# A hybrid decoder layer on one core: attention without the shifted copy of V, its remainders turned in 64x64 products

## The chip, the core and the metric

The kernel runs on one core of one Trainium2 chip, in one launch. The metric is the device time of a run in microseconds. A core has a matrix engine (TensorE, PE in the profile, with its weight loads as PEld), a vector engine (VectorE, DVE), an engine for activation functions (ScalarE, ACT), a general engine (GpSimd, POOL), an engine that issues transfers (SyncE, SP), and 16 DMA engines that serve the queues of SP, ACT and POOL. PE reads operands from SBUF and writes PSUM, 128 partitions in eight banks.

## The reference, cut to what matters

The layer projects x (2048 x 1024), runs an attention of 16 heads and a state-space mixer on the projections, gates and normalises both, and projects the result back. The change is in the attention, which is done for the dilations 1, 4 and 16 and then mixed by their log sums:

```python
def dilated_window_attention(q, k, v, slopes, dilation):
    # query t attends to t - j*dilation, j = 0..128; positions are split into
    # `dilation` residue sequences, each in blocks of 128; own and previous block
    scores = einsum('bnqrhe,bnkrhe->bnrhqk', qb, kk)
    valid = (jk >= 0) & (steps >= 0) & (steps <= ATT_STEPS)
    scores = where(valid, scores - slopes * steps * dilation, -inf)
    lse = logsumexp(scores, axis=-1)
    o = einsum('bnrhqk,bnkrhe->bnqrhe', exp(scores - lse), vv)
    return o, lse
...
    wts = softmax(stack([l1, l2, l3]), axis=0)
    y_att = wts[0] * o1 + wts[1] * o2 + wts[2] * o3
    y_att = rms_norm(y_att * silu(z_att), att_norm_g)
...
    out = einsum('bse,ed->bsd', concatenate([y_att, y_ssm], axis=-1), w_out)
    x = layer_norm(alpha * x + out, ln_g, ln_b)
```

All arithmetic is float32. A query in a block of 128 sees its own block up to itself and the previous block from the same place on.

## The kernel before, in words

Up to about 1148 us the kernel does the input projection and the mixer. It leaves q, k, v, the gate and the mixer's results in DRAM, and the output weights split in two parts (`d_wo`). The change leaves that alone.

**Pairs, dilations, units.** The attention then goes over eight pairs of heads (`pr`). A pair has three passes `d`: 0 for dilation 16, 1 for dilation 4, 2 for dilation 1. A pass has 16 blocks of 128 queries, in four groups `qd` of four; a *unit* (`pr, d, qd, half`) takes two of the four (`2 * i + half`, i = 0, 1), for both heads. There are 8 x 3 x 4 x 2 = 192 units. `first` (L902) says that a block has no previous block: all of dilation 16, the group `qd` = 0 of dilation 4, and block 0 of dilation 1.

**The window.** A block is worked in two halves `a` of 64 queries. With a previous block each half sees 192 keys: the first half those from two half blocks back, the second half those from one half block back. Of these, 128 are turned and multiplied as a whole, and 64 are left: the *remainder*. In the kernel before, both halves take the 192 keys in order of position (`keys`, L925), and the product of the first 128 with V needs 128 rows of V that start in the middle of a block for one of the halves. For that a second, shifted copy of V (`vs`, loaded at L880) stands beside V: row p of its block m is row p + 64 of V.

**The five steps of a unit.** `scores` (L935) multiplies q and k in 64x64 tiles (64 features of one head, 64 queries of one half), 192 or 128 columns each; head h writes its own PSUM bank. DVE adds the table of biases and takes the row minimum (L953). `exponentials` (L957) runs on ACT. `transposes` (L972) turns the probabilities on PE: four 128x128 transposes for the whole parts (L976), and, where a block has a remainder, two 128x128 transposes for the remainders (L984), which lie side by side in columns 128 to 256 because `cols` (L920) puts the second block's columns at the end of the tile. DVE copies both results to SBUF (PT L978, PC L987). `values` (L990) multiplies with V: products of 128 keys by 64 features (PT), then products of 64 keys (PC), which are added to the first. It accumulates into two PSUM tiles N0 and N1, one for each block index `i`; after two units ACT (or DVE) copies them out to `num` (L1022 to L1034).

**The order of the work** is written out by hand (L1254 to L1342): iteration i issues the scores of unit i, the transposes of unit i - 2 and the values of unit i - 3, in this order on PE. Between them, at fixed places `at` of the unit i - 3, stand the steps of the pair before: statistics to DRAM, `weights`, `broadcast` (L1083, on Sync's queue), `combine` (L1099, on POOL, for the last pair on DVE), and `keep_u` (L1095), which stores a pair's gated result in DRAM from a tile of the ring `wb` of three. A memset on DVE (L1087) opens each later use of this ring. V is loaded a pass at a time from POOL's or Sync's queue (L1302 to L1304, and the table STEPS at L1245).

**The output stage** (from L1343) computes the 16 row blocks of the result in two branches of eight 128x512 weights each, the mixer's (`br` = 1, weights 8 to 15) first. `load_w` (L1137) loads weights from POOL's queue into tiles that the attention has freed; LOADS (L1248) says where in the last pair each is loaded, `None` for a whole tile of 1 MB and 0 for the first half of it. The second halves of 12 to 15 are loaded behind the last unit (L1296). The last pair's broadcast and combination lie in this stage too, and the splits of the mixer's rows (L1159) stand behind them on DVE. PE's products of this stage are L1201 to L1203.

## Time and profile before

| what | value |
|---|---|
| median of three runs | 2009.96 us (2007.39 to 2012.77) |
| the profiled execution | 2003.82 us |
| its span, first to last instruction | 2002.0 us |
| mean granted PE clock | 0.991 |
| busy share of the span: PE, DVE, ACT, POOL | 97%, 64%, 56%, 50% |
| moved by DMA | 447.67 MB, 224 GB/s |

The profile is of one execution. Its times are microseconds from the span's start unless marked ns; L947 is line 947 of the kernel. A row of the timeline has the start, the length, the engine, the line, the operation, what it writes and reads, the shape, and how many instructions are merged in it; in brackets the engine's idle time before it and what ended that. A row of groups has the count, then busy time and mean ns of one, then the idle time before. PE's products are pipelined and their ends are modelled, so that PE can be busy without being at its peak; the distance from start to start says what a product occupies.

### The profile page before, as it was taken

How to read it: one execution, taken by the hardware profiler on the slowest of the kernel's cores; microseconds unless marked ns; L12 is line 12 of the kernel's file. 1: busy time of each engine (PE TensorE's matmuls, PEld its weight loads, DVE VectorE, ACT ScalarE, POOL GpSimd, SP SyncE). 2: the span in 40 equal slices, each digit the busy share in tenths (PEclk: the TensorE clock that was granted, in tenths of full speed). 3: DMA queues.
4: the chain of work that ended last, by engine and by line, in shares of the span. 5: the costliest groups of instructions: out<-in, count | busy, mean ns of one | idle time of the engine just before them, and what ended most of it. 6: DMA issues, size and time to landing. Idle time of an engine off the chain costs nothing.

```text
span 2002.0 us, 42714 instructions
## 1 busy us (share of the span) xinstructions
PE 1945.7 (97%) x16008; PEld 1588.2 (79%) x16008; DVE 1275.8 (64%) x3204; ACT 1120.0 (56%) x3036; POOL 998.3 (50%) x877
## 2 busy tenths in 40 slices
PE   8999999999999999999999999999999888999998
PEld 7888899888888888988888877777777666888886
DVE  7655376887766655644454388888887736655553
ACT  5454343566556774456566488988888732322220
POOL 0366514666556667155565343676776622432221
PEclk9999999999999999999999999999999998999999
DMA  6788676566787876888888766888888988332210
GB/s 270 236 284 293 213 280 227 159 195 190 237 306 266 279 245 239 312 269 256 272 277 259 256 228 165 229 244 235 252 238 254 265 242 260 134 102 92 92 61 32
DMA packets 260656, 447.67 MB, mean 224 GB/s; under 512 B 44785, under 2 KB 146673, under 8 KB 249057
## 3 DMA queue, kind: packets, MB, share of 16 engines
q1 hardware_dynamic: 170912, 205.39, 32.2%
q0 software_dynamic: 39088, 142.54, 21.6%
q10 hardware_dynamic: 50448, 97.01, 15.7%
q8 instruction: 126, 2.06, 0.4%
q14 instruction: 82, 0.66, 0.1%
HBM read 301.85 MB, written 151.39 MB: 226 GB/s over the span
## 4 chain that ended last, share of the span: by engine, by line
PE 85%; DVE 5%; DMA 4%; ACT 3%; issue 2%; POOL 1%; SPq 0%; ACTq 0%; DVEq 0%; POOLq 0%
PE pp L260 13%; PE pp L264 13%; PE pp L262 13%; PE N L1002 7%; PE S L947 6%; PE T L976 5%; PE pp L309 4%; PE S L1201 4%; PE S L1203 4%; PE S L1202 3%; PE ss L309 2%; PE T L1201 2%; PE T L1203 2%; PE T L1202 2%; PE ss L627 2%
## 5 line engine op out<-in xcount | busy, mean ns | idle before, releaser
L217 POOL TENSOR_TENSOR w<-wr,w 128x512 fp32r<-128x512 f32 x217 | 285.6, 1327 | 268.2 <-ACT w L216 184.0
L962 ACT ACTIVATE P<-P,st 128x192 f32<-128x192 f32 (+1 forms) x768 | 323.4, 423 | 59.9 <-DVE st L953 55.4
L252 ACT COPY ev<-pp 128x512 f32<-128x512 f32 x200 | 117.1, 587 | 315.3 <-PE pp L264 281.5
L953 DVE CUSTOM_DVE_ANT_0 P<-S,tb 128x192 f32<-128x192 f32 (+1 forms) x768 | 205.8, 324 | 53.6 <-PE S L947 44.1
L272 DVE TENSOR_TENSOR ev<-pp,ev 128x512 f32<-128x512 f32 x152 | 101.2, 686 | 140.6 <-PE pp L264 95.9
L216 ACT CAST w<-wr 128x512 fp32r<-128x512 f32 x224 | 134.1, 620 | 23.5 <-DVE wr L211 11.9
L962 ACT ACTIVATION_READ_ACCUMULATOR P<-P,st 128x1 f32 x768 | 145.0, 189 | 0.0
L1111 POOL TENSOR_TENSOR wb<-num,wb 128x2048 f32<-128x2048 f32 x21 | 95.7, 4558 | 93.7 <-DMA wb<-d_wd 90.2
L978 DVE COPY PT<-T 128x512 f32<-128x512 f32 x192 | 131.7, 686 | 3.8 <-PE T L976 3.8
L976 PE MATMUL T<-ident,P 128*128 128x128 f32 x768 | 127.3, 288 | 6.7 <-DVE PT L978 4.5
L1002 PE MATMUL N<-PT,v 128*64 128x64 f32 (+1 forms) x1536 | 124.5, 259 | 4.2 <-DVE PT L978 3.5
L976 PEld LDWEIGHTS T<-ident,P 128*128 128x128 f32 x768 | 81.3, 141 | 52.9 <-ACT P L962 16.8
L211 DVE TENSOR_TENSOR wr<-wr 128x512 f32<-128x512 f32 x128 | 112.2, 877 | 9.3 <-DMA wr<-w 5.9
L947 PE MATMUL S<-k,ex 64*64 64x192 f32 (+1 forms) x2048 | 108.8, 322 | 3.2 <-issue 3.2
L1002 PEld LDWEIGHTS N<-PT,v 128*64 128x64 f32 x1536 | 79.4, 138 | 38.3 <-issue 22.7
L459 DVE SCALAR_TENSOR_TENSOR ss<-U,cw,ss 128x512 f32<-128x512 f32 x144 | 106.0, 752 | 2.9 <-ACT ss L455 0.6
L1177 DVE TENSOR_REDUCE tb<-P 128x128 f32<-128x1024 f32 x30 | 60.2, 2006 | 45.1 <-ACT P L1174 21.1
L1239 POOL TENSOR_TENSOR k<-k,wb 128x1024 f32<-128x1024 f32 x8 | 25.8, 3225 | 122.0 <-DVE k L1238 122.0
L587 ACT ACTIVATE mt<-csb,wdr 128x128 f32<-128x128 f32 x256 | 78.9, 395 | 0.9 <-PE ss L627 0.8
L947 PEld LDWEIGHTS S<-k,ex 64*64 64x64 f32 x2048 | 66.4, 134 | 15.4 <-issue 8.9
L596 DVE TENSOR_TENSOR mt<-mt,ss 128x1024 f32<-128x1024 f32 x32 | 39.0, 1220 | 54.1 <-ACT mt L592 53.7
L260 PE MATMUL pp<-TT4h,w 128*128 128x512 f32 x176 | 69.6, 395 | 0.0
(493 smaller groups left out, 5991.1 us busy)
## 6 DMA issues: line engine op xcount, KB each, us to landing
wr<-w ACTq DMA_DIRECT2D x164, 256.0 KB
d_wc<-w SPq DMA_DIRECT2D x48, 512.0 KB
w<-d_wc POOLq DMA_DIRECT2D x48, 512.0 KB, 6.4
wb<-d_wd SPq DMA_DIRECT2D x48, 512.0 KB
d_wo<-wot POOLq DMA_DIRECT2D x32, 512.0 KB, 4.3
csb<-d_cs ACTq DMA_DIRECT2D x32, 512.0 KB
d_wv<-w SPq DMA_DIRECT2D x14, 1024.0 KB
w<-d_wv POOLq DMA_DIRECT2D x14, 1024.0 KB, 8.7
```

The costliest lines, as they stand in the source:

```text
L216: nc.scalar.copy(h, r)
L217: low.tensor_tensor(l, r, h.bitcast(F32), op=OP.subtract)
L260: nc.tensor.matmul(ps, w[:, 0, k], th[:, k], start=start and k == 0, stop=False, skip_group_check=not start)
L262: nc.tensor.matmul(ps, w[:, 0, k], tl[:, k], start=False, stop=False, skip_group_check=not start)
L264: nc.tensor.matmul(ps, w[:, 1, k], th[:, k], start=False, stop=(k == 3), skip_group_check=not start)
L309: nc.tensor.matmul(o, (th, tl)[j == 1][:, k, t], w[:, int(j == 2), k], start=start and r % 2 == k == j == 0, stop=(k == 3 and j == 2), ski ...
L947: nc.tensor.matmul(o, A["q"][d][64 * h:64 * h + 64, blk, 64 * a:64 * a + 64], kv, start=True, stop=True)
L953: nc.vector.tensor_tensor_reduce(P[:, h, cs], sp[h][:, cs], t, -0.125, 3.0e38, OP.add, OP.min, accum_out=stat(A, 0, d, h, blk))
L962: nc.scalar.activation(p, p, AF.Exp, bias=stat(A, 0, d, h, blk), scale=-1.0, accum_out=stat(A, 1, d, h, blk))
L976: nc.tensor.transpose(tp[:, h, i], P[:, h, 256 * i:256 * i + 128], ident)
L978: nc.vector.tensor_copy(pt, tp)
L1002: nc.tensor.matmul(o, l, r, start=start, stop=True, skip_group_check=True)
```

## The change

Six edits belong together:

- `keys` returns parts. Where a block has a previous one, the first half takes its 192 keys in order as before; the second half takes its own block (128 keys) first and the 64 keys of the previous block as a part of its own, written behind them. So both halves' first 128 columns belong to keys that start at a block of V. `scores` issues the first parts of both heads and halves, then the second parts. `cols` puts the second block's columns at 192, and the table of biases follows the new order.
- `transposes` turns the remainders in 64x64 products with a 64x64 piece of the identity, one for each head, block and half, with the result of half `a` in rows 64a to 64a + 63. They are plain products, not transposes.
- `values` keeps one accumulator for each half `a` in place of one for each block. First blocks of dilations 4 and 1 are done in two halves as well. The copies to `num` follow the new places.
- The shifted V and its loads go.
- `keep_u` is issued at (0, 0, 1) and not at (1, 0, 0).
- The three tiles of the shifted V take the weights 8, 9 and 10, in pairs 5 and 6; 11, 12 and 13 are loaded whole in the last pair, from its second pass on; 14 and 15 follow with their first halves, and the first half of weight 2 of the other branch. Behind the last unit only the second halves of 14 and 15 are left.

```diff
         def cols(d, qd, half, i):
-            w = 128 if first(d, qd, 2 * i + half) else 192
-            return slice(384 - w, 384) if i else slice(0, w)
+            return slice(192 * i, 192 * i + (128 if first(d, qd, 2 * i + half) else 192))
 
         def keys(A, d, qd, bq, h, a):
...
-            lo, hi = (j, j + 2 * w) if f else (j + w * (a - 2), j + w * (a + 1))
-            k = k[:, 4 * bq:4 * bq + 4, lo:hi] if d == 1 else k[:, :, lo:hi]
-            return k.rearrange("p r (c j) -> p c r j", j=4)
+            parts = [(0, j, j + 2 * w)] if f else [(0, j, j + 2 * w), (128, j - w, j)] if a else [(0, j - 2 * w, j + w)]
+            at = lambda lo, hi: k[:, 4 * bq:4 * bq + 4, lo:hi] if d == 1 else k[:, :, lo:hi]
+            return [(c, c + 64 * (hi - lo) // w, at(lo, hi).rearrange("p r (c j) -> p c r j", j=4)) for c, lo, hi in parts]
...
         def scores(A, d, qd, half):
...
-                for h in range(2):
-                    for a in range(2):
-                        o, kv = sp[h][64 * a:64 * a + 64, cs], keys(A, d, qd, 2 * i + half, h, a)
...
+                for n in range(2):
+                    for h in range(2):
+                        for a in range(2):
+                            for c0, c1, kv in keys(A, d, qd, 2 * i + half, h, a)[n:n + 1]:
+                                o = sp[h][64 * a:64 * a + 64, 192 * i + c0:192 * i + c1]
...
         def transposes(d, qd, half, P):
...
-            tc_ = psT.tile([128, 2, 2, 128], F32, name="T")
+            tc_ = psT.tile([128, 2, 2, 64], F32, name="T")
             for h in range(2):
-                nc.tensor.transpose(tc_[:, 0, h], P[:, h, 128:256], ident)
-            pc = io.tile([128, 2, 128], F32, name="PC", bufs=2)
-            rows = slice(64 * new[0], 128)
-            nc.vector.tensor_copy(pc[rows], tc_[rows, 0])
+                for i in range(new.start, new.stop):
+                    for a in range(2):
+                        r = slice(64 * a, 64 * a + 64)
+                        nc.tensor.matmul(tc_[r, h, i], P[r, h, 192 * i + 128:192 * i + 192], ident[r, r],
+                                         start=True, stop=True)
+            pc = io.tile([128, 2, 2, 64], F32, name="PC", bufs=2)
+            nc.vector.tensor_copy(pc[:, :, new], tc_[:, :, new])
...
         def values(A, d, qd, half, pts):
...
+                f = first(d, qd, 2 * i + half)
+                for a in range(2):
+                    for h in range(2):
+                        mm(out(i, h, a), v[:, m if f else m - 1 + a, 64 * h:64 * h + 64],
+                           pt[:, h, i, 64 * a:64 * a + 64], half == i == 0)
...
                 for a in range(2):
                     for h in range(2):
-                        w = (v, vs)[a != i][:, m - (a == i == 0 or a != i), 64 * h:64 * h + 64]
-                        mm(out(i, h, 64 * a, 64 * a + 64), w, pt[:, h, i, 64 * a:64 * a + 64], half == 0 and a == 0)
...
+                        r = slice(64 * a, 64 * a + 64)
+                        mm(out(i, h, a), v[r, at(2 * i + half) - a, 64 * h:64 * h + 64], pc[r, h, i], False)
...
-        LOADS = {(1, 0, 0): ((8, None, "k_0"),), (1, 1, 0): ((9, None, "q_0"),), (1, 2, 0): ((11, None, "vs"),),
-                 (1, 3, 0): ((12, 0, "q_1"), (13, 0, "v")), (2, 1, 0): ((10, None, "ex"),),
-                 (2, 2, 0): ((14, 0, "v"), (15, 0, "vs"))}
+        LOADS = {(5, 2, 1, 0): ((8, None, "vs"),), (6, 0, 1, 0): ((9, None, "vs"),), (6, 2, 1, 0): ((10, None, "vs"),),
+                 (7, 1, 0, 0): ((11, None, "k_0"),), (7, 1, 1, 0): ((12, None, "q_0"),), (7, 1, 3, 0): ((13, None, "q_1"),),
+                 (7, 2, 0, 0): ((14, 0, "v"),), (7, 2, 1, 0): ((15, 0, "v"),), (7, 2, 2, 0): ((2, 0, "ex"),)}
...
                         if pr == 7:
-                            for e in range(12, 16):
+                            for e in (14, 15):
                                 load_w(e, 1)
...
-                        load_v(pairs[pr], "v", 2, nc.sync)
-                        load_v(pairs[pr], "vs", 2, nc.sync)
+                        load_v(pairs[pr], 2, nc.sync)
...
-                    if pr > 1 and at == (1, 0, 0):
+                    if pr > 1 and at == (0, 0, 1):
                         keep_u(pairs[pr - 2], nc.sync)
...
-                    for e, name in enumerate(("num", "vs", "v", "wb", "num", "wb", "num")):
-                        load_w(1 + e, 0, name)
+                    for e, name in enumerate(("num", None, "v", "wb", "num", "wb", "num")):
+                        if name:
+                            load_w(1 + e, 0, name)
...
-        k = 64 * (p[:, None] // 64 + c[None, :] // 64 - 2) + kw[c % 64][None, :]
+        k = 64 * (p[:, None] // 64 + (c[None, :] // 64 + p[:, None] // 64) % 3 - 2) + kw[c % 64][None, :]
```

More of the change, by code (lines that the diff above doesn't have):

```diff
@@ L975, in transposes @@
                 for i in range(2):
-                    nc.tensor.transpose(tp[:, h, i], P[:, h, 256 * i:256 * i + 128], ident)
+                    nc.tensor.transpose(tp[:, h, i], P[:, h, 192 * i:192 * i + 128], ident)
             pt = io.tile([128, 2, 2, 128], F32, name="PT", bufs=4)
             nc.vector.tensor_copy(pt, tp)
-            new = [i for i in range(2) if not first(d, qd, 2 * i + half)]
-            if not new:
+            new = slice(int(first(d, qd, half)), 2 - int(first(d, qd, 2 + half)))
+            if new.start >= new.stop:
                 return pt, None
-            tc_ = psT.tile([128, 2, 2, 128], F32, name="T")
+            tc_ = psT.tile([128, 2, 2, 64], F32, name="T")
             for h in range(2):
-                nc.tensor.transpose(tc_[:, 0, h], P[:, h, 128:256], ident)
-            pc = io.tile([128, 2, 128], F32, name="PC", bufs=2)
-            rows = slice(64 * new[0], 128)
-            nc.vector.tensor_copy(pc[rows], tc_[rows, 0])
+                for i in range(new.start, new.stop):
+                    for a in range(2):
+                        r = slice(64 * a, 64 * a + 64)
+                        nc.tensor.matmul(tc_[r, h, i], P[r, h, 192 * i + 128:192 * i + 192], ident[r, r],
+                                         start=True, stop=True)
+            pc = io.tile([128, 2, 2, 64], F32, name="PC", bufs=2)
+            nc.vector.tensor_copy(pc[:, :, new], tc_[:, :, new])
             return pt, pc
@@ L996, in values, with out @@
                 A["N"] = [psN.tile([128, 512], F32, name=f"N{i}") for i in range(2)]
-            num, v, vs = A["num"][d], A["v"][d], A["vs"].get(d)
+            num, v = A["num"][d], A["v"][d]
             at = lambda bq: 4 * bq + qd if d == 1 else 4 * qd + bq
-            out = lambda i, h, lo, hi: A["N"][i][64 * h:64 * h + 64, 128 * half + lo:128 * half + hi]
+            def out(i, h, a=None):
+                if d == 0:
+                    return A["N"][i][64 * h:64 * h + 64, 128 * half:128 * half + 128]
+                c = 64 * (2 * i + half)
+                return A["N"][a][64 * h:64 * h + 64, c:c + 64]
             def mm(o, l, r, start):
@@ L1004, in values @@
                 m = at(2 * i + half)
+                if d == 0:
+                    for h in range(2):
+                        mm(out(i, h), v[:, m, 64 * h:64 * h + 64], pt[:, h, i], half == 0)
+                    continue
+                f = first(d, qd, 2 * i + half)
+                for a in range(2):
+                    for h in range(2):
+                        mm(out(i, h, a), v[:, m if f else m - 1 + a, 64 * h:64 * h + 64],
+                           pt[:, h, i, 64 * a:64 * a + 64], half == i == 0)
+            for i in range(2):
                 if first(d, qd, 2 * i + half):
-                    for h in range(2):
-                        mm(out(i, h, 0, 128), v[:, m, 64 * h:64 * h + 64], pt[:, h, i], half == 0)
                     continue
@@ L1010, in values @@
                     for h in range(2):
-                        w = (v, vs)[a != i][:, m - (a == i == 0 or a != i), 64 * h:64 * h + 64]
-                        mm(out(i, h, 64 * a, 64 * a + 64), w, pt[:, h, i, 64 * a:64 * a + 64], half == 0 and a == 0)
-            for a in range(2):
-                for i in range(2):
-                    m, rows = at(2 * i + half), slice(64 * i, 64 * i + 64)
-                    if first(d, qd, 2 * i + half):
-                        continue
-                    for h in range(2):
-                        w = v[rows, m - i] if a == i else vs[rows, m - 2 * i]
-                        mm(out(i, h, 64 * a, 64 * a + 64), w[:, 64 * h:64 * h + 64],
-                           pc[rows, h, 64 * a:64 * a + 64], False)
+                        r = slice(64 * a, 64 * a + 64)
+                        mm(out(i, h, a), v[r, at(2 * i + half) - a, 64 * h:64 * h + 64], pc[r, h, i], False)
             if half == 1:
@@ L1326, in hybrid_layer @@
                             if dd:
-                                load_v(pairs[pr + nx], x, dd[0])
+                                load_v(pairs[pr + nx], dd[0])
                             else:
@@ L1331, in hybrid_layer @@
                         permute(pairs[pr + 1], 1)
+                    if not half:
+                        for e, hf, name in LOADS.get((pr, d, qd, 0), ()):
+                            load_w(e, hf, name)
                     if pr < 7:
                         continue
-                    for e, hf, name in LOADS.get(at, ()):
-                        load_w(e, hf, name)
                     if at == (2, 0, 0):
```

39 lines of the change are left out of this document (17 added, 22 removed).

## The prediction

> **What bounds the kernel now.** I read the page first, then the stretches of the attention stage and of the output stage, then the timeline of one unit, and last the waits. The page gives the span and the chain that ended last:
>
> ```profile
> span 2002.0 us, 42714 instructions
> ...
> PE 85%; DVE 5%; DMA 4%; ACT 3%; issue 2%; POOL 1%; SPq 0%; ACTq 0%; DVEq 0%; POOLq 0%
> ```
>
> TensorE (PE) carries 85% of that chain. But the change touches only the attention (192 units from about 1148 to 1613 us) and the first 60 us of the output stage, so those two are read by themselves. The columns of the stretches are busy us and count of PE, PEld, DVE, ACT, POOL, then the granted clock, DMA share and GB/s:
>
> ```profile
> 1160.00:1613.00 453.00, 432.01 (x8135) 323.00 (x8135) 376.53 (x1877) 382.27 (x1697) 289.00 (x229) 0.98 0.80 232
> ...
> 1630.00:1640.00 10.00, 10.00 (x46) 8.12 (x45) 1.82 (x4) 4.54 (x6) 0.00 (x0) 1.00 1.09 325
> 1640.00:1650.00 10.00, 7.51 (x33) 5.80 (x31) 2.29 (x1) 0.00 (x0) 0.00 (x0) 1.00 1.02 237
> 1650.00:1660.00 10.00, 0.45 (x1) 0.45 (x2) 5.72 (x3) 0.47 (x1) 4.68 (x7) 0.60 1.19 255
> ```
>
> In the attention PE is idle for 21 us of 453, DVE for 76 and ACT for 71. A busy PE is not PE at its peak, so one steady unit of a second half (dilation 1, two blocks that each have a remainder) has to be read in order of time:
>
> ```profile
> 1420.73 0.83 PE L947 MATMUL S<-k,ex 64*64 64x192 f32 x16
> ...
> 1420.96 0.41 DVE L987 COPY PC<-T 128x256 f32<-128x256 f32 x1
> ...
> 1421.49 0.42 PEld L976 LDWEIGHTS T<-ident,P 128*128 128x128 f32 x4 [0.28 <-DVE PC L987]
> 1421.50 0.66 PE L976 MATMUL T<-ident,P 128*128 128x128 f32 x4
> ...
> 1421.99 0.38 PE L984 MATMUL T<-ident,P 128*128 128x128 f32 x2
> ...
> 1422.31 0.34 PE L1002 MATMUL N<-PT,v 128*64 128x64 f32 x4
> ...
> 1422.92 0.27 PE L1002 MATMUL N<-PC,v 64*64 64x64 f32 x2
> ...
> 1423.20 0.83 PE L947 MATMUL S<-k,ex 64*64 64x192 f32 x16
> ```
>
> The unit lasts 1423.20 - 1420.73 = 2.47 us and PE's four blocks fill it: scores 0.77 us, turning (L976 with L984) 0.81, values 0.61, remainders 0.28. The gap of 0.28 us in front of L976 is put down to DVE's copy of PC, but that copy ended at 1421.37, before L976 began: what shows is a pause that comes each time the tile size of the products changes (64x64, 128x128, 128x64, 64x64). So PE paces these units, and what is added to PE's work there is added to the time.
>
> **The change part by part.** *The remainders' turning.* Before, a unit turns its remainders in two 128x128 transposes (L984); after, in eight products of 64x64 with the identity. How many records such a product makes is seen in the groups kept apart by shape:
>
> ```profile
> L947 PE MATMUL S<-k,ex 64*64 64x192 f32 x1728 | 96.1, 329 | 1.8 <-issue 1.8
> L1002 PE MATMUL N<-PC,v 64*64 64x64 f32 x864 | 51.3, 233 | 0.0
> L1002 PE MATMUL N<-PC,vs 64*64 64x64 f32 x864 | 49.1, 233 | 1.2 <-issue 1.2
> L1002 PE MATMUL N<-PT,vs 128*64 128x64 f32 x864 | 45.3, 225 | 0.0
> L984 PE MATMUL T<-ident,P 128*128 128x128 f32 x224 | 43.8, 278 | 0.9 <-DVE PC L987 0.9
> ```
>
> By the code 104 units have two blocks with a remainder and 8 units have one (the first unit of dilation 1 in each pair); L984's 224 = 2 x 112 agrees. They ask for 104 x 8 + 8 x 4 = 864 remainder products, and there are 1728 records: each plain f32 product is two passes, while a transpose is one (224 records for 224 calls). A pass lengthens by some 53 ns for each 64 columns (225, 278 and 329 ns for 64, 128 and 192), and two transposes stand 0.38 - 0.27 = 0.11 us apart; so a pass occupies its tile for about 0.06, 0.11 and 0.16 us.
>
> The eight products are 16 passes of 64 columns on two tiles only, the two on the diagonal. The nearest row is the values block: 16 passes of 64 columns on two tiles (the two column halves), with a change of tile size behind it, 1422.31 to 1422.92 = 0.61 us. The two transposes that go occupied 0.22 us. So +0.39 us a unit; for a unit with one block, four pass times less, +0.16. Sum: 104 x 0.39 + 8 x 0.16 = 41.9 us. The lower bound is the remainder block: 16 passes on four tiles take 0.28 us; with a pause of 0.14 (the values block less eight passes, 0.61 - 8 x 0.058) that would be 0.42 - 0.22 = +0.20 a unit, 22 us. I take 41.9, as the diagonal has two tiles and not four.
>
> Here the Trainium skill speaks against the change: "TensorE: Matmul & The Clock Gate", section Terms, calls the transpose mode four times as fast for FP32. By that rule a 64-column product would cost four 64-column transposes, about 0.22 us, the eight of them on two tiles 0.88, and the part some 80 us instead of 41.9. The rows above say two passes at the same speed, so twice, and the sum keeps that.
>
> *The scores.* A block that has a remainder had four products of 192 columns; now the first halves keep 192, and the second halves have 128 and then 64. Four tiles work beside each other, and the two passes of one product don't hold up the next tile (sixteen passes of 0.16 us fit into 0.83). By tile, the first halves need 4 x 0.16 us as before, and the second 4 x 0.11 + 4 x 0.06: the same, or about 0.02 us more for the four extra passes, 104 x 0.02 = 2 us. Lower bound 0. Upper bound: the four extra passes run with nothing beside them, 0.21 us a unit, 22 us. I take 2, because the tiles are seen to run independently.
>
> *Values, accumulators, copies.* The count of value and remainder products stays, except that the 40 first blocks of the dilated passes are done in two halves: 40 x 0.01 = 0.4 us. Both accumulators are now needed within the first value products of a unit, not one of them later; the copies that free them end before that, and the values start 0.4 us later in a unit, so I cost it at nothing. The copies out keep their size (128x256) and change strides; ACT's 71 us of idle time cover that even if each took twice as long.
>
> *Shifted V goes.* Two loads of 1 MB a pair leave the GpSimd and Sync queues. No wait of PE on them shows in the attention, so directly nothing.
>
> *The u store, moved seven units earlier on Sync's queue.* It writes out the buffer that a later memset on DVE reuses, and that memset waits, with the score reductions of the unit queued behind it and PE behind these:
>
> ```profile
> 1548.50 1.79 SPq L1055 DMA_DIRECT2D d_st<-sT  x4
> 1554.52 0.38 SPq L1061 DMA_DIRECT2D cm<-d_st  x1
> 1554.95 0.54 SPq L888 DMA_DIRECT2D v<-d_v  x1
> 1555.58 2.49 SPq L888 DMA_DIRECT2D vs<-d_v  x1
> ...
> 1566.86 0.58 SPq L1096 DMA_DIRECT2D d_ua<-wb  x1
> ```
>
> ```profile
> DVE wb L1087 <- DMA d_ua<-wb: 9.4, 4, 2.6
> ...
> DVE P L953 <- ACT num L1033: 3.6, 8, 1.0
> DVE P L953 <- ACT P L962: 3.4, 10, 0.4
> ```
>
> The store takes the place on Sync's queue that the shifted V had (1555.6 for 1566.9), so what is behind it there, the table load, the weights' store and the first broadcast, sees one transfer of 1 MB as before. What it stores is ready by then:
>
> ```profile
> 1547.80 4.56 POOL L1125 TENSOR_TENSOR wb<-wb 128x2048 f32<-128x2048 f32 x1
> ```
>
> It starts 11 us earlier, four times the longest wait: the 9.4 us go, of which I take 8 as PE's share. The waits for ACT (3.6 + 3.4) shrink as each unit grows by 0.4 us: another 3. Bounds for the two together: 5 and 16.
>
> *Weights in freed tiles.* In pair 7 the GpSimd queue now has 1 MB instead of 2 MB of weights behind the end of the attention, and three tiles of 1 MB come one or two pairs sooner. What they compete with is the last pair's broadcast:
>
> ```profile
> 1646.81 2.29 DVE L1111 TENSOR_TENSOR wb<-num,wb 128x2048 f32<-128x2048 f32 x1 [9.23 <-DMA wb<-d_wd]
> 1653.74 2.29 DVE L1111 TENSOR_TENSOR wb<-num,wb 128x2048 f32<-128x2048 f32 x1 [4.64 <-DMA wb<-d_wd]
> ...
> 1659.55 0.80 PE L1203 MATMUL S<-k,num 128*128 128x512 f32 x1 [12.04 <-DVE num L1169]
> ```
>
> PE waits 12.0 us here for a split that DVE does behind the combination, which waits for the broadcast, at a time when the DMA engines are full (1.02 to 1.19 in the stretches above). 1 MB less at about 0.28 MB a us is 3.7 us; with a smaller wait for weights just before, I take 5. Below, it is 0, since the chain from the last unit to the broadcast stays; above, the whole 12 and 4 us of small waits ahead, 16.
>
> **The sum**, against the profiled execution (2003.8 us, 1.8 more than its span): 41.9 + 2 + 0.4 - 8 - 3 - 5 = +28. That execution lies 6.1 us below the median of the runs shown (2009.96), and I add the 28 to the median: 2038 us.
>
> **The rivals.** *One bank for both row halves* (8%). The eight products of a unit write both halves of one PSUM bank from both row halves of the array. In the rows of before, the two row halves always write two banks (S of each head, N of each block), so nothing shows whether they could share one. If they take turns, 16 passes stand one behind another: 0.46 us more a unit, 50 us more, 2088. The Trainium skill has this as a rule: "TensorEngine Tiling (Array Packing)", Gotcha 1: PSUM Pressure, says that different row tiles cannot use the same bank at once. No run here shows it yet.
>
> *Faster* (7%). The turning goes at its lower bound (22 us), and every wait of PE that touches DMA or ACT goes with the traffic: the 21 us of the attention and the 16 of the output stage. Then 2010 + 22 - 37 = 1995. It decides if a unit grows by less than 37 / 108 = 0.34 us. For it speaks that DMA is at 0.80 through the attention; against it, that few of those waits name a load that is dropped.
>
> *The extra work is covered* (5%). If DVE or ACT set the pace of the units, PE's 0.39 us would fall into their time and only the gains would be left against some extra: about 2010. Against it: both have over 70 us of idle time in 453, and the unit above is PE from end to end.
>
> **How the numbers follow.** The forecast has 80%. Its own bounds are 22 or 41.9 for the turning, 0 to 22 for the scores, -5 to -16 for the two queues, 0 to -16 for the tail; not all meet at once, and I give 2016 to 2062, which leaves out the first two rivals and most of the third. A change of 0.3% (6 us) is about what can be told from none. Faster 0.07, same 0.05, slower 0.88.
>
> **What would show it.** Right: a group of 1728 passes of T from P in 64x64, in pairs, with some 0.6 us from the first to the first value product; a steady unit of 2.85 to 2.90 us; no wait of DVE for the u store; score groups of 192, 128 and 64 columns that still take some 0.77 us a unit; PE's wait near the broadcast at 5 to 9 us. Wrong: a steady unit near 2.5 (turning covered), or above 3.2 (one bank, or scores in sequence), or an attention that grows while its steady units don't, by waits that aren't there now.

## The result, and the profile after

The changed kernel took 2069.86 us (median of 4 runs, 2067.12 to 2071.80); the kernel before, run beside it, 2008.80. The ratio is 1.0300, with an interval of 1.0280 to 1.0319: slower, as forecast, but by 61 us where 28 were forecast. The profiled execution took 2071.8 us, 68 more than the one before, which at 2003.8 lies 5 us below its kernel's median; the sums of stretches below are of these two executions.

The units themselves came out as predicted. The groups kept apart by shape (busy us, mean ns, idle before) have the passes that the prediction counted, and the second halves' scores as products of 128 and 64 columns:

```profile
L947 PE MATMUL S<-k,ex 64*64 64x192 f32 x864 | 98.5, 341 | 1.1 <-issue 1.0
...
L987 PE MATMUL T<-ident,P 64*64 64x64 f32 x1728 | 77.4, 229 | 1.8 <-issue 1.8
...
L947 PE MATMUL S<-k,ex 64*64 64x64 f32 x864 | 65.0, 223 | 3.6 <-issue 3.6
```

One steady unit in PE's timeline (start, length):

```profile
1431.21 0.90 PE L947 MATMUL S<-k,ex 64*64 64x192 f32 x24
1432.04 0.66 PE L976 MATMUL T<-ident,P 128*128 128x128 f32 x4
1432.62 0.68 PE L987 MATMUL T<-ident,P 64*64 64x64 f32 x16
1433.23 0.28 PE L1009 MATMUL N<-PT,v 128*64 128x64 f32 x2
```

The turning of the remainders (L987) occupies 1432.62 to 1433.23 = 0.61 us. The median distance from one such unit to the next is 2.88 us, against 2.47 before.

What is new stands between the units and within them, where PE stops. The stretch of the whole attention, before and after (busy us and count of PE, PEld, DVE, ACT, POOL; granted clock; DMA share; GB/s):

```profile
1148.40:1613.00 464.60, 443.61 (x8232) 328.92 (x8231) 382.74 (x1912) 391.19 (x1732) 300.56 (x247) 0.99 0.81 234
```

```profile
1145.60:1687.00 541.40, 505.58 (x10776) 408.73 (x10775) 383.16 (x1912) 393.61 (x1732) 289.44 (x239) 0.96 0.62 177
```

It grew by 77 us. The 104 full units account for 104 x 0.41 = 43. The rest goes with two signs: PE idles 36 us instead of 21, and the mean granted clock falls from 0.99 to 0.96. Among PE's waits in the attention (us in total, times, longest), before and after, these grew, and they name no tile and no engine:

```profile
PE S L947 <- issue: 3.5, 4, 1.4
...
PE N L1002 <- issue: 1.2, 2, 0.7
```

```profile
PE N L1009 <- issue: 17.6, 9, 3.5
PE S L947 <- issue: 7.5, 4, 3.1
...
PE T L987 <- issue: 1.8, 2, 1.5
```

"Issue" means that PE waited for nothing that the profile shows. One of these stops in PE's timeline, after a score block of which 4 of 24 products had run, and then the granted clock around it (the column before the DMA share):

```profile
1373.29 0.39 PE L947 MATMUL S<-k,ex 64*64 64x128 f32 x4
1376.58 1.33 PE L947 MATMUL S<-k,ex 64*64 64x128 f32 x16 [2.90 <-issue]
1377.84 1.11 PE L976 MATMUL T<-ident,P 128*128 128x128 f32 x4
```

```profile
1376.50:1378.00 1.50, 1.42 (x17) 1.30 (x18) 0.00 (x0) 0.00 (x0) 1.50 (x1) 0.50 1.01 208
1378.00:1380.00 2.00, 2.00 (x22) 1.55 (x23) 1.67 (x9) 1.59 (x8) 2.00 (x1) 0.50 1.04 229
1380.00:1382.00 2.00, 2.00 (x43) 1.88 (x46) 0.43 (x1) 0.44 (x4) 1.98 (x3) 0.50 1.03 209
```

So such a stop costs twice: 2.9 us of nothing, and then the turning transposes at 1.11 us instead of 0.66 while the clock is at half. Over the attention the clock record holds 47.8 us at 0.50, against 13.7 before. The sum nearly closes: 43 for the units, 26.9 - 5.1 = 22 for the stops, an estimated (47.8 - 13.7) / 2 = 17 for the half clock, less some 7 us of waits for DVE, ACT and GpSimd that went, make 75.

What PE waits for is its own program. The page lists a DMA queue of kind "instruction", before and after:

```profile
q8 instruction: 126, 2.06, 0.4%
```

```profile
q8 instruction: 146, 2.39, 0.5%
```

Its packets are 16 KB. PE has 16,008 matmul records before and 18,536 after, with as many weight loads: 32,016 and 37,072 instructions. 126 packets for the former are 64 bytes an instruction, and the 20 added packets for the 5056 added ones again 65. So this queue carries PE's instructions, 256 to a packet. The stops fit: the thirteen of over 0.6 us that are named issue, and two of 2.8 and 1.9 us that are put down to ACT, end 1.3 to 1.6 us after an instruction packet has landed. And they stand a whole number of packets apart. Counted in the trace, PE and its weight loads start 255 instructions from the end of one of these stops to the next in four cases, with one landing between, and 510 to 2541 in the others, always 254 to 256 for each landing between. So PE stops at the border of a packet, with nothing left to run. A full unit has 108 instructions before and 152 after, and PE needs a packet each 2.47 x 256 / 108 = 5.9 us before, each 2.88 x 256 / 152 = 4.9 us after.

The DMA queues don't always let one through in that time. Sync's (SP's) timeline around the stop shows four halves of the weights' broadcast asked for at once. Below it stand the DMA queues, by packets, MB and share of the 16 engines, in the 7.5 us before the fetch that ended the stop, then in the 2.7 us with it:

```profile
1362.66 3.65 SPq L1094 DMA_DIRECT2D wb<-d_wd  x4
```

```profile
q1 hardware_dynamic: 432, 1.55, 99.6%
```

```profile
q1 hardware_dynamic: 116, 0.45, 59.0%
q8 instruction: 1, 0.02, 2.6%
```

From 1366.4 to 1373.9 the broadcasts' queue q1 (it carries a table load of 128 KB as well) has the engines to 99.6%, and no instruction packet starts. In the packet records the fetches land at 1367.20 and 1375.10, 7.9 us apart, and PE goes on at 1376.58. A broadcast half is 64 rows of 8 KB, four packets of 0.57 us on each engine; four halves are 16 x 0.57 = 9 us.

The Trainium skill, "DMA: Bandwidth & Descriptors", section Queues, rings and completion order, says that each engine goes round the queues and drains some 9 to 17 descriptors of one before it switches; at 0.57 us each, with an 8 KB packet of the trace taken for a descriptor, that would be an estimated 5 to 10 us, and the trace's 7.9 lies in it. But q1 had nothing left when this fetch went through, so the trace doesn't tell such a turn from a wait for all that stood ahead. The Trainium skill's page "Runtime: NRT & Kernel Launch", section Instruction fetch mechanics, also has the blocks of 256 instructions, but calls their fetch mostly hidden; here the stops named "issue" are 26.9 us, and the measurement decides.

The last stage gained what was predicted. From the last value product to the end it took 389.1 us before and 383.1 after. PE's wait behind the broadcast shrank from 12.0 us, but only to:

```profile
1727.52 0.79 PE L1208 MATMUL S<-vs,num 128*128 128x512 f32 x1 [10.31 <-DVE num L1174]
```

### The profile page after: what moved, and what is told of

Same layout as the page of the kernel before. It is cut to its first block, busy times and chain, and to the rows that moved or that the text cites. A ratio compares the mean times of both kernels' runs of the same rounds, so it can differ in the third digit from the quotient of the medians.

```text
span 2070.0 us, 47743 instructions
## 1 busy us (share of the span) xinstructions
PE 2001.5 (97%) x18536; PEld 1662.6 (80%) x18536; DVE 1273.6 (62%) x3204; ACT 1121.0 (54%) x3036; POOL 985.6 (48%) x866
## 4 chain that ended last, share of the span: by engine, by line
PE 89%; DVE 3%; issue 3%; DMA 3%; ACT 2%; POOL 1%; SPq 0%; ACTq 0%; DVEq 0%; POOLq 0%
PE pp L260 13%; PE pp L264 13%; PE pp L262 13%; PE N L1009 8%; PE S L947 6%; PE T L976 5%; PE pp L309 4%; PE S L1206 3%; PE S L1208 3%; PE S L1207 3%; PE T L987 3%; PE ss L309 2%; PE T L1206 2%; PE T L1208 2%; PE T L1207 2%
## 5 line engine op out<-in xcount | busy, mean ns | idle before, releaser
L1009 PE MATMUL N<-PT,v 128*64 128x64 f32 (+1 forms) x2560 | 135.2, 245 | 10.2 <-issue 10.2
L1009 PEld LDWEIGHTS N<-PT,v 128*64 128x64 f32 x2560 | 100.8, 141 | 33.8 <-issue 15.3
L947 PE MATMUL S<-k,ex 64*64 64x192 f32 (+2 forms) x2912 | 114.6, 284 | 7.6 <-issue 7.5
L947 PEld LDWEIGHTS S<-k,ex 64*64 64x64 f32 x2912 | 98.0, 140 | 17.0 <-issue 12.4
L987 PEld LDWEIGHTS T<-ident,P 64*64 64x64 f32 x1728 | 61.4, 138 | 22.7 <-issue 16.8
L987 PE MATMUL T<-ident,P 64*64 64x64 f32 x1728 | 77.4, 229 | 1.8 <-issue 1.8
```

Source lines behind the costliest of these rows:

```text
L947: nc.tensor.matmul(o, A["q"][d][64 * h:64 * h + 64, blk, 64 * a:64 * a + 64], kv, start=True, stop=True)
L987: nc.tensor.matmul(tc_[r, h, i], P[r, h, 192 * i + 128:192 * i + 192], ident[r, r], start=True, stop=True)
L1009: nc.tensor.matmul(o, l, r, start=start, stop=True, skip_group_check=True)
```

## The experiments

Theory A: beside the longer units, the time is PE's program arriving late, because more instructions are wanted per microsecond while a fetch stands behind bursts of broadcast packets. Theory B, the first rival: an added instruction costs its own time on PE and no more, and the missing 33 us are waits for data that the new accumulators, the new loads or the earlier store bring. Theory C, a later rival within A: it is the amount of traffic, not its bunching. "Excess" below is worked out from the start of each unit's first score product: the time of each unit of pairs 1 to 6 above the shortest that the same unit took in any of these pairs, summed. Differences between kernels of different sets of runs are taken from their ratios, times 2008 us. The excess is 16.5 us before and 44.0 after; the shortest times sum to 319.6 and 351.2.

### One part undone at a time

The changed kernel with its remainders turned as before, by two 128x128 transposes for a unit:

```
-                for i in range(new.start, new.stop):
-                    for a in range(2):
-                        r = slice(64 * a, 64 * a + 64)
-                        nc.tensor.matmul(tc_[r, h, i], P[r, h, 192 * i + 128:192 * i + 192], ident[r, r], ...)
+                rem = P[:, h, 128:256] if both else P[:, h, 256:384]
+                nc.tensor.transpose(tc_[:, h].rearrange("p i c -> p (i c)"), rem, ident)
```

> The changed kernel with the remainders turned by two 128x128 transposes a unit, as before the change; everything else of the change stays. The blocks handed to the remainder products are the wrong ones, their number and size are the same. Theory A (the products cost 0.39 us of matrix work a unit, and their instructions make the matrix engine run out of program, because it reads its program in pieces of 256 instructions by DMA): a steady unit of 2.49 us, 28 instructions a unit fewer, so besides the 42 us the late pieces shrink by 10 to 20 us: 2008 to 2018 us in all. Theory B (the rest of the excess is data waits that the new accumulators, the new loads or the earlier store bring): only the 42 us go, 2028.

Measured: 2007.79, ratio to before 0.9999 (0.9988 to 1.0010). The unit is back at 2.48 us and the excess is 27.4. Turning is thus worth 60 us (0.0301 of 2008) and not 42: 18 us more than the prediction gave its products, while the accumulators, the loads and the early store stayed, which goes against B.

The changed kernel with the second halves' scores as one product of 192 columns:

```
-  parts = [(0, j, j + 2 * w)] if f else [(0, j, j + 2 * w), (128, j - w, j)] if a else [(0, j - 2 * w, j + w)]
+  parts = [(0, j, j + 2 * w)] if f else [(0, j + w * (a - 2), j + w * (a + 1))]
```

> The changed kernel with the second halves' scores as one product of 192 columns in order of position (the table of biases and V then belong to other columns: the window is computed wrongly). It takes 16 instructions out of a unit and hardly any matrix time. Theory A: the steady unit is the same to 0.03 us, but the stalls at the borders of 256 instructions shrink by 8 to 15 us: 2053 to 2062. Theory B: 2067 to 2070.

Measured: 2053.18, ratio 1.0216 (1.0193 to 1.0240), so this part is worth 17 us. Yet the shortest units sum to only 1.9 us less than in the changed kernel (the prediction's 2 for all pairs stands), and the excess falls by 12.5, to 31.5. The 16 instructions that it adds to a unit cost more than the time that they take.

### Instructions alone, in the kernel before

Eleven products of one column, written to unused columns, in each unit with a remainder in its second block: 44 instructions more a unit, as in the changed kernel, and none of its data flow.

```
+            if d and not first(d, qd, 2 + half):
+                for n in range(11):
+                    h, a = n // 2 % 2, n % 2
+                    nc.tensor.matmul(sp[h][64 * a:64 * a + 64, 500:501], A["q"][d][...], A["k"][..., 0, 0:1], ...)
```

> The kernel before with eleven more products of one column (64x64 weights) ahead of the scores of each unit that has a remainder: 44 instructions a unit more, as the change adds, and nothing else of the change. Their results are not read. Theory A: a steady unit of 2.70 to 2.80 us (25 to 35 us in all) and, beyond that, 15 to 25 us more of stalls at the borders of 256 instructions: 2050 to 2068. Theory B: only their own time, 2034 to 2044, with the stalls as before.

Measured: 2075.37, ratio 1.0343 (1.0324 to 1.0361). The direction is A's, but the size is above both: the unit grew to 2.81 us, a little more than forecast, and the excess is 47.4. PE's waits look like those of the changed kernel:

```profile
PE S L943 <- issue: 8.4, 9, 2.9
PE N L1008 <- issue: 7.4, 3, 2.7
PE S L953 <- issue: 5.7, 5, 1.5
...
PE T L990 <- issue: 3.5, 1, 3.5
```

So the stops need nothing of the change's data flow: more instructions for PE are enough.

### No broadcasts

The changed kernel without the broadcast transfers of pairs 0 to 6:

```
             for h in range(2):
+                if A["pr"] < 7:
+                    continue
...
-                eng.tensor_tensor(wb, A["num"][d], wb, op=OP.mult)
+                eng.tensor_tensor(wb, A["num"][d], wb if last else A["num"][d], op=OP.mult)
```

> The changed kernel without the broadcast transfers of pairs 0 to 6 (their combinations multiply by the numerators themselves in place of the weights; the memset, the program of the matrix engine and all else stay). Theory A, now with its cause: a piece of program comes late where it stands behind the broadcasts in the DMA engines. Then the stalls that end with a piece's arrival fall from 33 us to under 8, the half-clock stretches behind them go too, and the time is 2029 to 2043. If the pieces are late by their number alone, whatever else is transferred: 2062 to 2070.

Measured: 2018.24, ratio 1.0065 (1.0047 to 1.0084): 47 us less than the changed kernel by the ratios, more than A gave. The units are as long (2.88), the excess is 6.8, and no half clock is left in the attention, though the table load that shares their queue stays. The waits:

```profile
PE N L1009 <- issue: 1.5, 2, 1.1
PE T L987 <- issue: 1.1, 1, 1.1
PE S L947 <- issue: 1.0, 2, 0.9
```

With PE's program on time the extra products keep the length that the prediction gave them. The total grows by less, 13 us, because waits of the kernel before are gone too: PE's waits in the attention sum to 4 us here and to 21 there, and its half clock was 13.7 us.

### Shorter rows

Each half cut into four transfers of 512 columns, so that a packet is 2 KB and not 8, in the changed kernel and in the kernel before:

```
+                for c in range(0, S, 512):
+                    nc.sync.dma_start(f2(wb[64 * h:64 * h + 64])[:, c:c + 512],
+                                      dap(d_wd[A["pr"]], (d * 2 + h) * S + c, [[0, 64], [1, 512]]))
```

> The changed kernel with each broadcast transfer cut into four of 512 columns: rows of 2 KB in place of 8 KB, the same bytes, 24 transfers a pair in place of 6. If a piece of program waits until a run of rows of another queue is through, the run is a quarter as long, and the stalls fall by half or more: 2040 to 2056. If it waits for all that was issued before it: 2067 to 2072. More issues on Sync's queue cost nothing by either.

Measured: 2041.15, ratio 1.0175 (1.0154 to 1.0196), 25 us less than the changed kernel; the excess is 18.6, PE's waits for nothing shown fall to 15 us and its half clock to 6.8. But the edit did a second thing, which its expectation put at nothing. Four issues for a half take Sync some four times as long, so the halves leave about 3 us apart:

```profile
1475.62 11.52 SPq L1095 DMA_DIRECT2D wb<-d_wd  x16
```

That is four halves in 11.5 us, where the changed kernel sends them in 3.65. So this run doesn't tell what the shorter packets are worth from what the spacing is.

> The kernel before with the same cut of the broadcasts. It has 6 us of stalls that end with a piece's arrival and two half-clock stretches in the attention. Short rows as a cure: 2000 to 2005. Waiting for all that was issued: 2007 to 2010.

Measured: 2029.94, ratio 1.0128 (1.0104 to 1.0152): slower by 25 where a gain or nothing was expected. PE's waits tell why:

```profile
PE S L947 <- POOL ex L912: 8.9, 7, 2.7
...
PE N L1002 <- issue: 0.2, 1, 0.2
```

The stops for the program are gone (0.2 us), but PE now waits for GpSimd's copies of q (`ex`). GpSimd's timeline has the copy behind the last step of the combination, whose inputs are the broadcasts:

```profile
1505.98 4.54 POOL L1127 TENSOR_TENSOR wb<-wb 128x2048 f32<-128x2048 f32 x1
1510.45 2.78 POOL L912 COPY ex<-q 128x256 f32<-128x256 f32 x8
```

Here too the four issues space the halves: the sixth leaves 16 to 19 us after the first, where it was 11 to 12. The fetches pass, the broadcast is later, and all that is queued behind it on GpSimd is later too. In the kernel before, that costs more than its few stops.

### The store of u

The early store alone, put into the kernel before, and the late one, put back into the changed kernel. The edit is the same line in both, in opposite directions:

```
-                    if pr > 1 and at == (1, 0, 0):
+                    if pr > 1 and at == (0, 0, 1):
                         keep_u(pairs[pr - 2], nc.sync)
```

> The kernel before with the one edit of the u store: issued at (0, 0, 1) in place of (1, 0, 0). As predicted, the four waits of the memset for it (9.4 us) go and the time falls by 5 to 9 us, 2000 to 2004. If two of the stalls that I put down to the memset were the matrix engine's own late program pieces (it sat idle for 1.4 us at 1518 and at 1575 with nothing named), it falls by 3 to 5 us only.

Measured: 2014.36, ratio 1.0034 (1.0017 to 1.0052), slower by 6.6 us where A had it faster. The excess is 32.6 instead of 16.5. Sync's queue in the kernel before, and then in this one, in pair 7:

```profile
1565.68 1.12 SPq L1089 DMA_DIRECT2D wb<-d_wd  x2
1566.86 0.58 SPq L1096 DMA_DIRECT2D d_ua<-wb  x1
1567.49 10.45 SPq L1089 DMA_DIRECT2D wb<-d_wd  x4
```

```profile
1579.93 8.28 SPq L1089 DMA_DIRECT2D wb<-d_wd  x6
```

The memset's wait for u had been spreading the broadcasts over 12 us. Without it six halves leave in 8, and the program is later behind them: PE's waits for nothing shown are 11.0 us at the values alone, where the kernel before has 1.2. In the whole attention they rise from 5 to 18.5 us and the half clock from 13.7 to 37.5, while PE's waits for DVE fall from 10.2 to 1.8: there was a gain, and more than the gain was lost.

> The changed kernel with the u store back at (1, 0, 0), after the first broadcast. By the run of that edit alone (+6.6 us on the kernel before) it should fall by 4 to 12 us, 2058 to 2066: the memset's wait then parts the broadcasts and a piece of program can pass. If the edit is worth what I predicted, it rises by 6 to 9, 2076 to 2079.

Measured: 2069.07, ratio 1.0312 (1.0288 to 1.0335). Neither of the two ranges: in the changed kernel the place of this store is worth nothing that shows (its ratio was 1.0300, 1.0280 to 1.0319). The first four halves leave over some 7 us here instead of 3, with the store's 1 MB between them, and PE's waits for nothing shown stay at 26.8 us. So it isn't enough to part the halves by another large transfer.

### Spacing the broadcasts

Each half gets a small memset of its own, and the halves are placed in six units instead of three, so that Sync's queue waits for VectorE to reach the unit. First in the changed kernel and in the kernel before:

```
+        SPACED = {(0, 3, 0): (0, (0,)), (0, 3, 1): (0, (1,)), (1, 0, 1): (1, (0,)), (1, 1, 0): (1, (1,)),
+                  (1, 2, 0): (2, (0,)), (1, 2, 1): (2, (1,))}
...
+            for h in halves:
+                if A["pr"] < 7:
+                    nc.vector.memset(wb[64 * h:64 * h + 64, 0, 0:1], 0.0)
+                nc.sync.dma_start(f2(wb[64 * h:64 * h + 64]), ...)
...
-                    if pr and at in ((0, 3, 0), (1, 0, 1), (1, 2, 0)):
-                        broadcast(pairs[pr - 1], d + (at == (1, 2, 0)))
+                    if pr and at in SPACED:
+                        broadcast(pairs[pr - 1], *SPACED[at])
```

> The changed kernel, with the two halves of each pair's three broadcasts asked for one unit apart (each half waits in SyncE's queue for a small memset that VectorE reaches in its own unit), so that four halves never stand in the DMA rings together; nothing else changes, all the work is done. Theory A (the added time over the added passes is PE's program arriving late behind a burst of broadcast packets): a half is 64 rows of 8 KB, four packets on each of 16 rings, 4 x 0.57 = 2.3 us, instead of 16 and some 9 us before a fetch gets through; most of the excess of 27 us over the pairs, and of the half clock behind it, goes: 2030 to 2050. Theory C (it is the amount of broadcast and load traffic beside the fetch, not its bunching, that makes the fetch late): 2062 to 2075, as the changed kernel.

Measured: 2056.05, ratio 1.0255 (1.0225 to 1.0285): between A and C, with an excess of 33.4. This run decides nothing, for it did not do what it set out to:

```profile
1357.98 0.36 SPq L1086 DMA_DIRECT2D d_wd<-cm  x1
1360.97 5.73 SPq L1096 DMA_DIRECT2D wb<-d_wd  x4
```

Sync issues the weights' store at 1357.98 and can send the first half only once it has landed, at 1360.97; by then VectorE has passed two memsets, and four halves still leave in 5.7 us.

> The kernel before, with the same spacing of the broadcasts and nothing else. By theory A its own late fetches, some 6 us of PE's stops and the half clock behind them, go: 1995 to 2004, which beats both kernels. If the later second halves hold GpSimd's combination up, so that a load or copy behind it on GpSimd is late for PE: 2010 to 2025, with PE's waits for the copies of k or for a load in place of its waits for nothing shown. Theory C: no change, 2003 to 2010.

Measured: 2011.26, ratio 1.0018 (1.0007 to 1.0029): 3.5 us slower. The edit did not space the halves here either: in Sync's rows they leave in pairs as in the kernel before, and only the sixth is 2 us later.

The early store of u and this spacing together, in the kernel before:

> The kernel before, with u stored early as the change stores it and with the halves of the broadcasts asked for one unit apart; all the work is done. The early store alone made this kernel 6.6 us slower, the spacing alone 3.6 us slower. Theory A with the burst (the early store took VectorE's wait for u away, 9 us in the trace, and paid for it with six broadcast halves in one burst, behind which PE's fetches stood): with both the wait is gone and the burst too, 1998 to 2006, and it beats both kernels. If spacing does not help, the two costs add: 2014 to 2020. If VectorE's wait was never on the path and the early store merely moved traffic: 2008 to 2013.

Measured: 2013.42, ratio 1.0037 (1.0024 to 1.0049). The costs neither add nor cancel; it stands where the early store alone stands. In six of the seven pairs the first four halves leave within 3 us, so nothing was spaced.

Short rows and this spacing together, in the changed kernel:

> The changed kernel with short rows (2 KB, as in the run that cut them) and the halves one unit apart, together; all the work is done. Theory A: a fetch then has at most four packets' worth of one half's short rows ahead of it in a turn, and what was left with either alone goes: 2025 to 2040, near the 2018 without broadcasts. If short rows make the broadcasts themselves later, so that GpSimd's combination and what stands behind it are late for PE, the second spacing adds to that: 2042 to 2056. If the two remedies do not add: 2040, as short rows alone.

Measured: 2046.86, ratio 1.0182 (1.0156 to 1.0207): no better than short rows alone, and in the range of the second case. The excess is 25.5. The halves leave as far apart as with short rows alone, so there was nothing for the spacing to add.

Then the halves placed later, so that each really waits for its unit, with the first two steps of GpSimd's combination one unit later, and with them the loads of the next pair's q and k:

```
+        SPACED = {(0, 3, 0): (0, (0,)), (1, 0, 1): (0, (1,)), (1, 1, 0): (1, (0,)), (1, 1, 1): (1, (1,)),
+                  (1, 2, 0): (2, (0,)), (1, 2, 1): (2, (1,))}
...
-        STEPS = {(1, 0, 0): (0, "q", 1),
-                 (1, 1, 0): (1, "k", 1), (1, 2, 0): ...
+        STEPS = {(1, 0, 1): (0, "q", 1),
+                 (1, 1, 1): (1, "k", 1), (1, 2, 0): ...
```

> The changed kernel with each broadcast half behind a memset of its own unit, from the unit on in which the weights have landed, and the first two steps of GpSimd's combination half a block later, so that SyncE's rows show one half at a time, some 2.5 us apart; all the work is done. Bunching (theory A): the excess over the pairs, 44 us in the changed kernel and 33 with the spacing that was only partly one, falls to 10 to 20: 2022 to 2042. Amount (theory C): the six halves still fill the rings for some 14 us of each pair, and a fetch meets them there all the same: 2048 to 2060, as with the partial spacing.

Measured in the changed kernel: 2033.86, ratio 1.0132 (1.0112 to 1.0152), 34 us less than the changed kernel with the same work and the same bytes. Sync's rows show the spacing, four halves in 9.1 us and then two in 3.2:

```profile
1413.61 9.13 SPq L1096 DMA_DIRECT2D wb<-d_wd  x4
...
1425.08 3.16 SPq L1096 DMA_DIRECT2D wb<-d_wd  x2
```

From 1413.6 to 1430.0 the DMA queues let three instruction packets through, one in 5.5 us, though q1 has the engines to 75%:

```profile
q1 hardware_dynamic: 671, 2.75, 75.0%
...
q8 instruction: 3, 0.05, 1.3%
```

PE's waits in the attention, and its stretch:

```profile
PE S L947 <- issue: 4.1, 5, 1.2
PE N L1009 <- issue: 2.9, 4, 1.1
...
PE T L976 <- issue: 0.6, 2, 0.4
```

```profile
1145.50:1643.50 498.00, 487.71 (x10774) 393.90 (x10775) 379.86 (x1940) 392.86 (x1732) 290.18 (x239) 0.99 0.67 192
```

The excess is 14.7 us, the clock is back at 0.99, the unit is still 2.88 us. The bytes are the same and the stops go, so C falls. That it is the bunching, and not the steps and loads that moved along, rests on the run with short rows too: it moved none of them, had its halves as far apart, and lost its stops in good part.

> The kernel before with the same one-at-a-time broadcasts; u is stored where it was. Bunching: 1996 to 2004, its own late fetches gone. Amount, or a combination that ends later and holds back GpSimd's copies and loads: 2008 to 2018.

Measured: 2011.24, ratio 1.0020 (1.0009 to 1.0030). But here the halves did not come one at a time. In six of the seven pairs the second, third and fourth leave within 1.3 to 2 us of each other; in this one between 1402.0 and 1403.3:

```profile
1396.90 0.49 SPq L1091 DMA_DIRECT2D wb<-d_wd  x1
1397.45 0.58 SPq L1098 DMA_DIRECT2D d_ua<-wb  x1
1398.25 5.06 SPq L1091 DMA_DIRECT2D wb<-d_wd  x3
```

PE's waits for nothing shown are 11 us instead of 5.

> The kernel before with u stored early and one broadcast half at a time. If the early store is worth the 9 us of VectorE's wait once no burst follows it: 1992 to 2000, and faster than the same kernel with the late store by 4 to 9. If VectorE's wait was hidden all along: within 2 us of the kernel with the late store. If the early store costs by itself: over 3 us slower than that.

Measured: 2013.43, ratio 1.0031 (1.0018 to 1.0043). The early store is worth nothing here: 2 us more than with the late one, which the intervals don't tell apart. In this run too the first three halves leave within 1.3 to 2.2 us in six of the seven pairs. So these two runs don't test what real spacing would bring the kernel before. The one run of it whose halves did leave some 3 us apart is that of the short rows, and there the stops went (0.2 us) and the combination was late. None of the versions beats the kernel before.

## Why the prediction was right or wrong

**Turning, right as time on PE.** The block takes 0.61 us, from the row of the values as the prediction had it, and the unit grew from 2.47 to 2.88 us where 2.85 to 2.90 was predicted. The shortest units of six pairs grew by 31.6 us, 5.3 a pair, where 41.9 + 2.4 for eight pairs is 5.5 (its own terms give 41.8). By the run with two transposes the whole part is worth 60, the rest being stops. The rule of the Trainium skill ("TensorE: Matmul & The Clock Gate", Terms), by which the block would have been 0.88 us, does not hold here: 16 passes in 0.61 us are two for each product, not four. The rival of one bank fell as well: with both row halves writing into one bank the passes start in pairs, 8 ns apart, a pair each 58 ns, and the block is as long as the values block, which works on two column halves. What the Trainium skill has in "TensorEngine Tiling (Array Packing)", Gotcha 1, costs nothing that this trace shows.

**Scores, right as time on PE.** The 2 us were confirmed by the run with whole scores, whose shortest units are 1.9 us less over six pairs; with the stops, the part is worth 17.

**Weights in freed tiles, right in size, in part by luck.** -5 was forecast and -6.0 measured in the last stage. But PE's wait near the broadcast, from which most of it was to come, is 10.3 us, above the 5 to 9 that were named, and so gives only 1.7. The rest lies between the attention's end and this wait, and its cause wasn't looked for.

**The store of u, wrong.** The memset's wait for it left the list of DVE's waits, as predicted, but the time did not follow. -8 was taken as PE's share of 9.4. In the trace before, PE waits right behind two of the four memsets, as here, by 1.7 and 1.2 us, and behind the other two by 0.2 at most:

```profile
1406.63 0.06 DVE L1087 MEMSET wb<- 128x1 f32 x1 [2.42 <-DMA d_ua<-wb]
1408.56 0.63 PE L976 MATMUL T<-ident,P 128*128 128x128 f32 x4 [1.74 <-DVE PT L978]
```

So some 3 us were PE's share by that trace. And the runs show +6.6 in the kernel before, 0 in the changed one, and +2 where the broadcasts were spaced. The step asked where a stall goes and answered "nowhere"; in the kernel before, what came next was the broadcast burst that the stall had been holding apart. The -3 for DVE's waits for ACT has no ground in the runs either: these waits are 16.5 us in the changed kernel, where they were 7.

**The sum, wrong in what it left out.** The step that failed is "PE paces these units, and what is added to PE's work there is added to the time": it counted PE's passes as time on the array, and not as instructions that must be brought in, so the fetch of PE's program stood in the sum at nothing. Forecast for the attention was 41.9 + 2 + 0.4 - 8 - 3 = +33, measured +77. The stops and their half clock are some 39 us of it. The last sentence of the prediction, an attention that grows while its steady units don't, by waits that aren't there now, named the sign but not the cause. Its row was on the page (q8, 126 packets), and 0.4% of the DMA engines is no measure of what a late packet costs.

With the broadcasts one at a time the changed kernel stands at 1.0132, where the forecast of 2038 on 2010 was 1.014: its attention is +33.4 us and its last stage -5.5. That match is in part luck, for it is not quite the forecast's own sum. The longer units give +43, and some 10 us of gains stand beside them. They go with PE's waits for DVE, ACT and GpSimd, which total 15 us in the attention before and 2 there; some 3 of these stood behind the memset, not the 8 for u.

Open is what real spacing would bring the kernel before, which has 5 us of these stops: the runs that meant to space its broadcasts left two to four halves together. In the run with one half at a time its excess is 24.5 us instead of 16.5, but the trace of 16.5 is the fast execution of 2003.8, so part of this is the draw of the trace. Open too is what the size of the packets does by itself, and whether the place of the loads of q and k behind the broadcasts matters; neither was tried alone.

## What to carry to other kernels

Count the instructions that an edit adds as well as their time: work out how long a packet of the program lasts in the stage, and compare it with the longest stretch in which other transfers hold all the DMA rings. A small stop of a tensor engine that runs without pause costs its length and can bring several microseconds of half clock behind it. Before a wait is taken away, look at what its end lets loose, for a wait in front of large transfers may be the only thing that keeps them apart.

## What the runs showed of the hardware

- PE's instructions come by DMA in 16 KB packets of 256. PE ran out at about 1373.7, 6.5 us after the last packet had landed, which at 152 instructions in 2.88 us is an estimated 340 instructions (344 in the trace); so at that landing it held less than one packet beside the new one. A stop that follows another directly comes 255 instructions later.
- In the stop shown a fetch landed 7.9 us after the one before it, behind packets of 8 KB on another queue, where PE needs one each 4.9 us. With the same bytes in halves 2.5 to 3 us apart, PE's waits for nothing shown fall from 27 to 8 us, and without the broadcasts to 4.
- Ten of the stops in the changed kernel's attention, of 1.5 to 3.5 us each, came with a granted clock of 0.50 for 3.4 or 6.8 us.
- A product of one column is not free: 44 instructions of them lengthened a unit by 0.34 us.
- Two row halves of the array writing into one PSUM bank, on their own partitions, lost no time that shows: 16 passes in 0.61 us, where one behind another they would take an estimated 16 x 0.058 = 0.93.
